# Twelve short products by zero in two feed-forward stages and four by zero ahead of two waits of TensorE

## The chip, the cores and the metric

The kernel runs on one core of a Trainium2 chip. The metric is the device time of one execution in microseconds (us). Its engines each run one queue of instructions in order: PE is TensorE (matrix products; PEld is its weight load), DVE is VectorE, ACT is ScalarE, POOL is GpSimd, SP is SyncE, which here issues the DMAs.

## What is computed

A two-layer decoder trunk over 256 positions of width 1024: layer 0 is a gated linear recurrence and a SwiGLU feed-forward, layer 1 is attention on shared keys and values and a second SwiGLU feed-forward; each is preceded by an RMS norm whose shift and scale come from a conditioning vector. Cut to what matters here:

```python
def rmsnorm(x, g):
    return x * lax.rsqrt(jnp.mean(x * x, axis=-1, keepdims=True) + RMS_EPS) * g

def swiglu(h, w_gate, w_up, w_down):          # 1024 -> 2816 -> 1024
    return (jax.nn.silu(h @ w_gate) * (h @ w_up)) @ w_down

for l in range(2):
    if l == 1:
        kv = shared_kv(x, shift, scale, kv_norm, w_kv)
    h = modulate(rmsnorm(x, norm_mix[l]), sh_m, sc_m)
    x = x + g_m * (rglru_mixer(h, ...) if l == 0 else moba_mixer(h, w_q, w_o, *kv, rel_bias))
    h = modulate(rmsnorm(x, norm_ffn[l]), sh_f, sc_f)
    x = x + g_f * swiglu(h, w_gate[l], w_up[l], w_down[l])
return rmsnorm(x, final_norm)
```

## The kernel before

**Products.** Activations lie transposed, 128 channels by 256 positions a tile. Most 128x128x256 products are done split: weight and activation are each cut into a high part and a rest (`whi`, `wlo` and `h`, `l`; ACT makes the high part, L439, DVE the rest, L440), and `mm3` issues three products in the fp32r format, high by high, high by rest, rest by high (L387 to L389). A product of plain float32 operands (L449, L544) comes as two records in the trace. Two feed-forwards, `f0` and `f1`, are built by `ffn`: `f_g`, 32 tiles (four output tiles `g00` to `g03`, k = 0 to 7) on the not yet normed input, while the sum of squares `f_st` (L544, five products against a tile of ones) is taken; then `f_p`, 320 tiles (ten steps i of two halves q, two j, eight k); then `f_d`, 176 tiles (eight outputs m, 22 k). `f_g` of `f0` is plain float32 (L449), that of `f1` is split. Steps of `f_p` are multiplied into `f` and split into `ah` and `al` (L606, L607) for `f_d`. Between the feed-forwards stand `kp`, `vp`, `qp` (keys, values, queries), the scores, `op` (probabilities by values) and `ao` (output projection); ahead of `f0`, `wo` (output projection of the recurrence) and `sh_f0`, a conditioning vector by 64 narrow float32 products on the PE (L477).

**Order.** Nothing of the order is written by hand. Every operation is handed to a planner, `Plan` (L93), with a rank: its number in the program, plus an amount by engine and name out of two tables, `KN` and `PRIO`. `Plan.run` (L153) keeps a clock for each engine and places, step by step, the ready operation that can start first, and among those the one of lowest rank; SBUF and PSUM slots (four for `whi`, four for `wlo`, four for raw weights, three for rows of conditioning weights `mraw`, eight PSUM banks) are given out in the same pass. The result is one fixed order for each engine; at run time an engine waits at the instruction that stands first in its queue, whatever stands behind it. One operation more, or one that takes longer in the planner's clock, can so move others on all engines.

Of the kernel before, what the change touches and what calls it, by code (L numbers as in the profile page):

```python
# [318 lines left out]
def build(tc, t):  # L319
    nc = tc.nc  # L320
    ctx = ExitStack()
    with ctx:
# [17 lines left out]
        slots("mraw", MRN, D)  # L340
        pool.tile([P, 16], F32, name="shift", tag="shift")
        slots("t2", T2N, 2 * S, KN["t2r"])
# [39 lines left out]

        def mm3(cost, out, wh, wl, xh, xl, start, stop, R, Wr, skip=False):
            def fn():
                o = out()
                h_, l_, a_, b_ = wh(), wl(), xh(), xl()
                nc.tensor.matmul(o, h_, a_, start=start, stop=False, skip_group_check=skip)  # L387
                nc.tensor.matmul(o, h_, b_, start=False, stop=False, skip_group_check=skip)  # L388
                nc.tensor.matmul(o, l_, a_, start=False, stop=stop, skip_group_check=skip)  # L389
            return pe(cost, fn, R, Wr)  # L390

# [18 lines left out]
        ones = own([P, P], "ones")  # L410
        dve(P, 0.0005, lambda: nc.vector.memset(ones.ap, 1.0), (), (ones,))
        warm = own([P, 1], "warm")
# [29 lines left out]

        def gemm(out, key, wu, o, xu, start, stop, skip=False, w=P, n=S, cost=0.3275):

            ps, c = out
            hi, lo = wu
            xh, xl, xo = xu
            if hi is None:
                pe(n * 0.0016875 + 0.002, lambda: nc.tensor.matmul(  # L449
                    ps.ap[:, c:c + n], lo.ap[:, o:o + w], xh.ap[:, xo:xo + n], start=start, stop=stop,  # L450
                    skip_group_check=skip), (lo, xh if n > S else (xh, xo)), ((ps, key),))
                return
            mm3(cost, lambda: ps.ap[:, c:c + n], lambda: hi.ap[:, o:o + w], lambda: lo.ap[:, o:o + w],
                lambda: xh.ap[:, xo:xo + n], lambda: xl.ap[:, xo:xo + n], start, stop,
                (hi, lo) + ((xh, xl) if n > S else ((xh, xo), (xl, xo))), ((ps, key),), skip)

# [8 lines left out]
        def mod_cols_pe(name, src, bias, g=None):  # L465

            ps = PS(name + "_ps")
            for u in range(4):
                raw = pl.buf("raw", f"{name}_r{u}")
                load(raw, CU, lambda raw=raw: raw.ap, src[u])  # L470
                for kk in range(2):
                    k = 2 * u + kk

                    def fn(k=k, kk=kk, raw=raw):
                        for q in range(4):
                            o = kk * D + q * S
                            nc.tensor.matmul(ps.ap[32 * q:32 * q + 32, :S], csr.ap[:, 32 * k:32 * k + 32],  # L477
                                             raw.ap[:, o:o + S], start=(k == 0), stop=(k == KC - 1),
                                             tile_position=(0, 32 * q))
                    pe(0.52, fn, (raw, csr), (ps,))  # L480
# [214 lines left out]
        def head_front(h):  # L695
# [43 lines left out]
            vv_.append(v_)  # L739

        def head_y(h):
            if h < NYH:
                ps = xps[NH_LRU + h]
            else:
                pl.bias = KN["ypsum"]
                ynat = h >= NH_LRU - 0
                wu = unit(t["win_y"][h - NYH], 2048, f"wiy{h}", ynat)
                ps = PS(f"yb{h}")
                pl.bias = KN["y"]
                for j in range(2):  # L750
                    for k in range(KC):
                        gemm((ps, j * S), 0, wu, (j * KC + k) * P, (hf[k], hf[k], 0) if ynat else hx(h0, k), k == 0,
                             k == KC - 1)
            pl.bias = KN["y"]
            y_ = T2(f"y{h}")
            act(2 * S, lambda: nc.scalar.activation(y_.ap, ps.ap, AF.Copy), (ps,), (y_,))
            ys.append(y_)
# [90 lines left out]
        def ffn(l, xs, a, sh, g, name, rates):  # L848
# [9 lines left out]
            shc = None if nat else shift_cols(sh, name)  # L858
            gp0 = [PS(f"{name}_g0{i}") for i in range(4)]
            wu = None  # L860
            for k in range(KC):
# [28 lines left out]
            for i in range(1, FT // 2):  # L890
                pq = [PS(f"{name}_p{i}{q}") for q in range(2)]
                wq = [unit(t[f"ffb{l}"][2 * (i - 1) + q], 2048, f"{name}b{i}{q}") for q in range(2)]
                if i == 1:
                    for k in range(KC):
                        for q in range(2):
                            for j in range(2):
                                gemm((pq[q], j * S), 0, wq[q], (j * KC + k) * P, hx(h, k), k == 0 and j == 0,
                                     k == KC - 1, skip=True)
                else:
                    for q in range(2):  # L900
                        for j in range(2):
                            for k in range(KC):
                                gemm((pq[q], j * S), 0, wq[q], (j * KC + k) * P, hx(h, k), k == 0, k == KC - 1)
                step(0)
# [6 lines left out]
            for m in range(KC):  # L911
                ps = PS(f"{name}_d{m}")
                for half in range(2):
                    wu = unit(t[f"ffc{l}"][2 * m + half], 11 * P, f"{name}c{m}{half}")
                    for kk in range(11):
                        k = half * 11 + kk
                        gemm((ps, 0), 0, wu, kk * P, hx(aa, k), k == 0, k == FT - 1)
                step(1)
# [172 lines left out]
        for u in range(4):  # L1091
# [3 lines left out]
            for m in range(KC):  # L1095
                for k in range(2):
                    gemm((acc[m // 2], (m % 2) * S), 0, wu, k * 1024 + m * P, (oh, ol, k * S),
                         u == 0 and k == 0 and m % 2 == 0, u == 3 and k == 1, skip=True)
        x3 = [residual(x2[k], acc[k // 2], (k % 2) * S, 0, mods["g_m1"], k, "x3") for k in range(KC)]

# [136 lines left out]
```

## Time and profile before

| | |
|---|---|
| time, three runs | 610.31, 613.24, 615.05 us; median 613.24 us |
| the profiled execution's own time | 608.61 us |
| its span, first to last instruction | 606.8 us |
| PE busy | 585.9 us, 97% |
| DVE, ACT busy | 471.8 us (78%), 340.6 us (56%) |
| DMA | 162.94 MB, mean 269 GB/s |
| f0, its products of f_p and f_d | 152 to 329 us of the span |
| f1, its products of f_p and f_d | 430 to 598 us of the span |

The profiled execution is one of its own and lies 4.6 us below the median of the three runs. A row of the trace gives the start within the span, the busy time, the engine, the line and operation, output and input, the shape and the count; in square brackets the idle time of the engine ahead of it and what ended it.

### The profile page before, as it was taken

Reading aid. Unit: us, or ns where it says so; the run is one execution under the profiler, and the core shown is the slowest. Engines: PE = TensorE matmul, PEld = TensorE weight load, DVE = VectorE, ACT = ScalarE, POOL = GpSimd, SP = SyncE. Lnnn points to the kernel's source line nnn. Section 1 sums busy time; section 2 is a strip of 40 time slices with the busy share of each in tenths; the row PEclk is TensorE's granted clock in tenths of the full one; section 3 lists DMA queues with packets and bytes.
Section 4 is the critical chain, followed back from the end, with each engine's and each line's share of the span. In section 5 each row is a group of like instructions: output and inputs, shape, how many; then the busy total and the mean of one; then the engine's idle time right before and its main releaser. Section 6 shows DMA issues by size and latency. Waiting matters only on the chain.

```text
span 606.8 us, 11423 instructions
## 1 busy us (share of the span) xinstructions
PE 585.9 (97%) x4706; PEld 563.2 (93%) x4706; DVE 471.8 (78%) x743; ACT 340.6 (56%) x509; POOL 1.2 (0%) x10
## 2 busy tenths in 40 slices
PE   3999989999999999999999999998999999999996
PEld 1999868998999999999999889998999999999996
DVE  6998788977997898788878969889997654545542
ACT  6537898718653443343336899747664444434432
POOL 0000000000000000000000000000000000000000
PEclk9999999999999999999999999999999999999999
DMA  8996999795988899798979538786686654445501
GB/s 307 353 339 239 332 355 355 278 383 224 350 312 323 336 348 323 257 334 315 377 295 357 203 143 322 282 332 245 218 306 274 214 203 165 144 144 192 191 1 70
DMA packets 33362, 162.94 MB, mean 269 GB/s; under 512 B 3700, under 2 KB 4893, under 8 KB 23966
## 3 DMA queue, kind: packets, MB, share of 16 engines
q1 hardware_dynamic: 33310, 162.21, 72.2%
q8 instruction: 37, 0.61, 0.4%
q14 instruction: 15, 0.12, 0.1%
HBM read 161.14 MB, written 1.06 MB: 267 GB/s over the span
## 4 chain that ended last, share of the span: by engine, by line
PE 63%; DMA 18%; DVE 12%; ACT 3%; issue 3%; SPq 0%; DVEq 0%; ACTq 0%
PE ps_f_p L388 11%; PE ps_f_p L387 11%; PE ps_f_p L389 11%; PE ps_f_d L388 3%; PE ps_f_d L389 3%; PE ps_f_d L387 3%; PE ps_ga L449 3%; DMA mraw_mr_sh_kv_m__2730<-in_kvmod 2%; DVE wlo_f0c_l L440 2%; DMA raw_sh_f_r<-in_modp 1%; DMA mraw_mr_g_m_m__3469<-in_mod 1%; DMA raw_wix<-in_win_x 1%; PE ps_qp L389 1%; PE ps_qp L388 1%; PE ps_qp L387 1%
## 5 line engine op out<-in xcount | busy, mean ns | idle before, releaser
L388 PE MATMUL ps_f_p<-t_f_l,whi_f0b_h 128*128 128x256 f32 x320 | 89.7, 280 | 0.0
L387 PE MATMUL ps_f_p<-t_f_h,whi_f0b_h 128*128 128x256 f32 x320 | 89.5, 280 | 0.0
L389 PE MATMUL ps_f_p<-t_f_h,wlo_f0b_l 128*128 128x256 f32 x320 | 89.3, 279 | 0.0
L389 PE MATMUL ps_f_p<-t_f_h,wlo_f1b_l 128*128 128x256 f32 x320 | 88.5, 276 | 0.0
L387 PE MATMUL ps_f_p<-t_f_h,whi_f1b_h 128*128 128x256 f32 x320 | 88.4, 276 | 0.0
L388 PE MATMUL ps_f_p<-t_f_l,whi_f1b_h 128*128 128x256 f32 x320 | 88.4, 276 | 0.0
L388 PEld LDWEIGHTS ps_f_p<-t_f_l,whi_f0b_h 128*128 128x128 f32 x320 | 60.1, 188 | 0.2 <-DVE t_f_l L568 0.2
L387 PEld LDWEIGHTS ps_f_p<-t_f_h,whi_f0b_h 128*128 128x128 f32 x320 | 60.2, 188 | 0.0
L389 PEld LDWEIGHTS ps_f_p<-t_f_h,wlo_f1b_l 128*128 128x128 f32 x320 | 60.1, 188 | 0.1
L388 PEld LDWEIGHTS ps_f_p<-t_f_l,whi_f1b_h 128*128 128x128 f32 x320 | 60.1, 188 | 0.0
L387 PEld LDWEIGHTS ps_f_p<-t_f_h,whi_f1b_h 128*128 128x128 f32 x320 | 60.1, 188 | 0.0
L389 PEld LDWEIGHTS ps_f_p<-t_f_h,wlo_f0b_l 128*128 128x128 f32 x320 | 59.8, 187 | 0.0
L440 DVE TENSOR_TENSOR wlo_f1b_l<-raw_f1b_r,whi_f1b_h 128x2048 fp32r<-128x2048 f32 x20 | 45.6, 2289 | 18.1 <-ACT whi_f1b_h L439 18.1
L439 ACT ACTIVATE whi_f1b_h<-raw_f1b_r 128x2048 fp32r<-128x2048 f32 x20 | 38.2, 1912 | 24.8 <-issue 11.9
L439 ACT ACTIVATE whi_f0b_h<-raw_f0b_r 128x2048 fp32r<-128x2048 f32 x20 | 38.2, 1910 | 21.5 <-issue 19.1
L388 PE MATMUL ps_f_d<-t_f_al,whi_f0c_h 128*128 128x256 f32 x176 | 49.2, 280 | 0.8 <-DVE t_f_al L607 0.8
L389 PE MATMUL ps_f_d<-t_f_ah,wlo_f0c_l 128*128 128x256 f32 x176 | 49.3, 280 | 0.0
L387 PE MATMUL ps_f_d<-t_f_ah,whi_f0c_h 128*128 128x256 f32 x176 | 49.1, 279 | 0.0
L440 DVE TENSOR_TENSOR wlo_f0b_l<-raw_f0b_r,whi_f0b_h 128x2048 fp32r<-128x2048 f32 x20 | 45.6, 2287 | 4.2 <-ACT whi_f0b_h L439 4.1
L389 PE MATMUL ps_f_d<-t_f_ah,wlo_f1c_l 128*128 128x256 f32 x176 | 48.6, 276 | 0.0
L387 PE MATMUL ps_f_d<-t_f_ah,whi_f1c_h 128*128 128x256 f32 x176 | 48.6, 276 | 0.0
L388 PE MATMUL ps_f_d<-t_f_al,whi_f1c_h 128*128 128x256 f32 x176 | 48.6, 276 | 0.0
(469 smaller groups left out, 1661.3 us busy)
## 6 DMA issues: line engine op xcount, KB each, us to landing
raw_f0b_r<-in_ffb SPq DMA_DIRECT2D x20, 1024.0 KB, 6.9
raw_f1b_r<-in_ffb SPq DMA_DIRECT2D x20, 1024.0 KB, 4.9
raw_f0c_r<-in_ffc SPq DMA_DIRECT2D x16, 704.0 KB, 5.9
raw_f1c_r<-in_ffc SPq DMA_DIRECT2D x16, 704.0 KB, 4.0
raw_wix<-in_win_x SPq DMA_DIRECT2D x8, 768.0 KB, 6.7
raw_wout_r<-in_wout SPq DMA_DIRECT2D x5, 1024.0 KB, 9.9
raw_wiy_r<-in_win_y SPq DMA_DIRECT2D x4, 1024.0 KB, 6.0
raw_sh_f_r<-in_modp SPq DMA_DIRECT2D x4, 1024.0 KB, 6.1
```

Of the source, the lines that this page charges most:

```text
L387: nc.tensor.matmul(o, h_, a_, start=start, stop=False, skip_group_check=skip)
L388: nc.tensor.matmul(o, h_, b_, start=False, stop=False, skip_group_check=skip)
L389: nc.tensor.matmul(o, l_, a_, start=False, stop=stop, skip_group_check=skip)
L439: act(n - o, lambda: nc.scalar.activation(hi.ap[:, o:n], raw.ap[:, o:n], AF.Copy), (raw,), (hi,))
L440: tt(n - o, lambda: nc.vector.tensor_sub(lo.ap[:, o:n], raw.ap[:, o:n], hi.f[:, o:n]), (raw, hi), (lo,))
L449: pe(n * 0.0016875 + 0.002, lambda: nc.tensor.matmul(ps.ap[:, c:c + n], lo.ap[:, o:o + w], xh.ap[:, xo:xo + n], start=start, stop=stop, sk ...
```

## The change

Two tiles of zeros and ones exist already or are made at the start: 16 columns of an unused tile are set to zero (`zero`), beside `ones` (128x128). `mm3` gets a flag `lead`: with it, one plain float32 product of `ones` by the 16 columns of `zero` is issued ahead of the three products, and added into the first 16 columns of the same output (the sum is unchanged, since it adds zero). In each feed-forward six tiles have it: of `f_p` i = 1 at k = 5 (q = 0, j = 0) and i = 4, 7, 10 at k = 1 (q = 0, j = 0), of `f_d` m = 1 and 4 at k = 1. `between` issues four plain float32 products of `zero` by the identity (16x128) into a PSUM tile that is overwritten later: one ahead of `sh_f0`, after a product `yb` of the recurrence, one ahead of `f_g` of `f1`, after the last product of `ao`. Both carry a rank of 1000 less than their number. The tables are unchanged. Lines behind the edits move by 2 to 23.

```diff
-        def mm3(cost, out, wh, wl, xh, xl, start, stop, R, Wr, skip=False):
+        def mm3(cost, out, wh, wl, xh, xl, start, stop, R, Wr, skip=False, lead=False):
             def fn():
                 o = out()
+                if lead:
+                    nc.tensor.matmul(o[:, :16], ones.ap, zero.ap, start=False, stop=False, skip_group_check=True)
                 h_, l_, a_, b_ = wh(), wl(), xh(), xl()
                 nc.tensor.matmul(o, h_, a_, start=start, stop=False, skip_group_check=skip)
...
+        zero = pl.buf(None, "zero", tile=zt)
+
+        def fixed():
+            nc.vector.memset(ones.ap, 1.0)
+            nc.vector.memset(zero.ap, 0.0)
+        dve(P, 0.0005, fixed, (), (ones, zero))
...
+        def between(ps, last):
+
+            def fn():
+                for i in range(4):
+                    nc.tensor.matmul(ps.ap[0:16, :P], zero.ap, ident.ap, start=True, stop=True)
+            pe(0.05, fn, (zero, ident), ((ps, 0),), after=[last], rank=-1000)
...
+            if name == "sh_f0":
+                between(ps, ybs[2,0,2])
...
+            if l == 1:
+                between(gp0[0], ao_last)
...
                                 gemm((pq[q], j * S), 0, wq[q], (j * KC + k) * P, hx(h, k), k == 0 and j == 0,
-                                     k == KC - 1, skip=True)
+                                     k == KC - 1, skip=True, lead=k == 5 and q == 0 and j == 0)
...
-                                gemm((pq[q], j * S), 0, wq[q], (j * KC + k) * P, hx(h, k), k == 0, k == KC - 1)
+                                gemm((pq[q], j * S), 0, wq[q], (j * KC + k) * P, hx(h, k), k == 0, k == KC - 1,
+                                     skip=i in (4, 7, 10) and q == 0 and j == 0 and k == 1, lead=i in (4, 7, 10) and q == 0 and j == 0 and k == 1)
...
-                        gemm((ps, 0), 0, wu, kk * P, hx(aa, k), k == 0, k == FT - 1)
+                        gemm((ps, 0), 0, wu, kk * P, hx(aa, k), k == 0, k == FT - 1, skip=m in (1, 4) and k == 1, lead=m in (1, 4) and k == 1)
```

The planner's result moves with it. Three places, before and after.

First, ACT where `f0` ends and the keys begin. `whi_wv0` and `whi_wv4` are the high parts of the two weight units of the values, `n2_sq0` to `n2_sq7` the squares of the eight tiles for the norm that the keys need. Before:

```order
L439 ACTIVATE whi_wv0_h_3700<-raw_wv0_r_3612 128x2048
L595 ACTIVATE t1_kv_u1_h_3746<-kv_sh_172 128x2
L599 ACTIVATE t1_kv_u1_h_3746<-t1_f0x_1_3236,sc_kv_m_158 128x256
L595 ACTIVATE t1_kv_u2_h_3749<-kv_sh_172 128x2
L599 ACTIVATE t1_kv_u2_h_3749<-t1_f0x_2_3315,sc_kv_m_158 128x256
L530 ACTIVATE t1_n2_sq0_3767<-t1_f0x_0_3138 128x256
L530 ACTIVATE t1_n2_sq1_3769<-t1_f0x_1_3236 128x256
L530 ACTIVATE t1_n2_sq2_3771<-t1_f0x_2_3315 128x256
L530 ACTIVATE t1_n2_sq3_3773<-t1_f0x_3_3403 128x256
L530 ACTIVATE t1_n2_sq4_3775<-t1_f0x_4_3492 128x256
L439 ACTIVATE whi_wv4_h_3777<-raw_wv4_r_3644 128x2048
L530 ACTIVATE t1_n2_sq5_3797<-t1_f0x_5_3577 128x256
```

With the change:

```order
L446 ACTIVATE whi_wv0_h_3713<-raw_wv0_r_3584 128x2048
L446 ACTIVATE whi_wv4_h_3751<-raw_wv4_r_3629 128x2048
L546 ACTIVATE t1_n2_sq0_3759<-t1_f0x_0_3151 128x256
L546 ACTIVATE t1_n2_sq1_3763<-t1_f0x_1_3245 128x256
L546 ACTIVATE t1_n2_sq2_3765<-t1_f0x_2_3331 128x256
L546 ACTIVATE t1_n2_sq3_3767<-t1_f0x_3_3424 128x256
```

All eight squares now stand behind the second high part. On the PE the five products `n_st` on those squares now stand right behind the last product of `f_d`, and all 96 products of `kp` behind them; before, 33 products of `kp` stood ahead of them, twelve of these between the last ones of `f_d`.

Second, DVE where attention ends and `f1` begins. `ol4` and `ol6` are the rests that the products of `ao` read (of heads 4 and 5, and 6 and 7), `mr_sh_f1_m` are rows of conditioning weights that come by DMA. Before:

```order
L440 TENSOR_TENSOR wlo_wo_3_l_4697<-raw_wo_3_r_4252,whi_wo_3_h_4495 128x2048
L1077 TENSOR_TENSOR t2_ol4_4573<-ps_op5_4703,t2_oh4_4552 128x256
L1077 TENSOR_TENSOR t2_ol6_4724<-ps_op6_4712,t2_oh6_4718 128x256
L462 SCALAR_TENSOR_TENSOR mraw_mr_sh_f1_m__4687,sh_f1_m_170<-mraw_mr_sh_f1_m__4687,csb_130 128x1024
L1077 TENSOR_TENSOR t2_ol6_4724<-ps_op7_4716,t2_oh6_4718 128x256
L462 SCALAR_TENSOR_TENSOR mraw_mr_sh_f1_m__4710,sh_f1_m_170<-mraw_mr_sh_f1_m__4710,csb_130 128x1024
```

With the change:

```order
L476 SCALAR_TENSOR_TENSOR mraw_mr_sh_f1_m__4672,sh_f1_m_170<-mraw_mr_sh_f1_m__4672,csb_130 128x1024
L1099 TENSOR_TENSOR t2_ol4_4710<-ps_op4_4541,t2_oh4_4700 128x256
L1099 TENSOR_TENSOR t2_ol4_4710<-ps_op5_4690,t2_oh4_4700 128x256
L476 SCALAR_TENSOR_TENSOR mraw_mr_sh_f1_m__4692,sh_f1_m_170<-mraw_mr_sh_f1_m__4692,csb_130 128x1024
L1099 TENSOR_TENSOR t2_ol6_4735<-ps_op6_4702,t2_oh6_4720 128x256
L476 SCALAR_TENSOR_TENSOR mraw_mr_sh_f1_m__4698,sh_f1_m_170<-mraw_mr_sh_f1_m__4698,csb_130 128x1024
L447 TENSOR_TENSOR wlo_f1a0_l_4752<-raw_f1a0_r_4396,whi_f1a0_h_4626 128x2048
L447 TENSOR_TENSOR wlo_f1a4_l_4775<-raw_f1a4_r_4504,whi_f1a4_h_4686 128x2048
L476 SCALAR_TENSOR_TENSOR mraw_mr_sh_f1_m__4750,sh_f1_m_170<-mraw_mr_sh_f1_m__4750,csb_130 128x1024
L1099 TENSOR_TENSOR t2_ol6_4735<-ps_op7_4793,t2_oh6_4720 128x256
L447 TENSOR_TENSOR wlo_f1b10_l_4801<-raw_f1b10_r_4644,whi_f1b10_h_4782 128x2048
```

Each rest now has a DMA's row ahead of it, the last one two units of weights besides. On the PE `op7` stands 36 products ahead of the end of `ao` (before: 84), and behind `ao` stand the four products of `between`, all five `f_st` and only then `f_g` (before: one `f_st`, twelve products of `f_g`, four `f_st`).

Third, PE and DVE at the end of `f_p` of `f1`: `g03` is the fourth output tile of `f_g`, `al0` the rest that the first products of `f_d` read. On the PE with the change:

```order
L391 MATMUL ps_f1_p101_6260<-t2_f1_h3_5170,wlo_f1b101_l_6170 128x256
L389 MATMUL ps_f1_g03_4952<-t1_f1_u7_h_5011,whi_f1a4_h_4686 128x258
L390 MATMUL ps_f1_g03_4952<-t1_f1_u7_l_5020,whi_f1a4_h_4686 128x258
L391 MATMUL ps_f1_g03_4952<-t1_f1_u7_h_5011,wlo_f1a4_l_4775 128x258
L389 MATMUL ps_f1_d0_6346<-t2_f1_ah0_6332,whi_f1c00_h_6204 128x256
```

On DVE there, with the change:

```order
L930 TENSOR_TENSOR t2_f1_f10_6320<-ps_f1_p101_6260,t2_f1_s10_6278 128x512
L905 TENSOR_TENSOR t1_f1_tu1_6324<-ps_f1_g03_4952,t1_f1_rstd_4897 128x256
L895 COPY f1_bs_195<-ps_f1_g03_4952 128x1
L907 SCALAR_TENSOR_TENSOR t2_f1_f0_5192<-t1_f1_tu1_6324,f1_bs_195,t1_f1_tg1_5176 128x256
L447 TENSOR_TENSOR wlo_f1c10_l_6330<-raw_f1c10_r_6133,whi_f1c10_h_6322 128x1408
L447 TENSOR_TENSOR wlo_f1c11_l_6336<-raw_f1c11_r_6196,whi_f1c11_h_6328 128x1408
L623 TENSOR_TENSOR t2_f1_al0_6340<-t2_f1_f0_5192,t2_f1_ah0_6332 128x512
```

Before, the last three products of `g03` stood at the start of `f1`, behind the first six of `f_p`, and `al0` on DVE ahead of the fourth step of `f_p`; now `g03` stands behind all of `f_p`, and `al0` behind it and two units of weights.

## Rows read from the trace of the kernel before

**Rows 1.** The page: the span and the first busy line.

```profile
span 606.8 us, 11423 instructions
PE 585.9 (97%) x4706; PEld 563.2 (93%) x4706; DVE 471.8 (78%) x743; ACT 340.6 (56%) x509; POOL 1.2 (0%) x10
```

**Rows 2.** Waits of the PE: who waited for whom, us in total, times, longest.

```profile
PE ps_f_st L544 <- DVE t_f_sq L539: 2.3, 2, 2.1
PE ps_sh_f_ps L477 <- DMA raw_sh_f_r<-in_modp: 2.2, 1, 2.2
PE ps_kp L388 <- DVE t_kv_u_l L601: 0.9, 1, 0.9
PE ps_f_d L388 <- DVE t_f_al L607: 0.8, 1, 0.8
```

**Rows 3.** Stretches of PE: us, busy (products), granted clock, DMA share, GB/s.

```profile
160.00:260.00 100.00, 100.00 (x852) 1.00 0.87 317
450.00:550.00 100.00, 100.00 (x884) 1.00 0.56 198
```

**Rows 4.** Timeline of PE: a short stop in f0 and one in f1.

```profile
273.15 0.38 PE L388 MATMUL ps_f_d<-t_f_al,whi_f0c_h 128*128 128x256 f32 x1 [0.78 <-DVE t_f_al L607]
...
434.31 0.38 PE L389 MATMUL ps_f_p<-t_f_h,wlo_f1b_l 128*128 128x256 f32 x1
```

**Rows 5.** Timeline of PE near the end: the narrowest float32 products.

```profile
598.76 0.50 PE L1121 MATMUL ps_n_st<-ones,t_n_sq 128*128 128x1 f32 x4
599.12 0.96 PE L1125 MATMUL ps_ty<-ident,t_y 128*128 128x128 f32 x7
```

**Rows 6.** Timeline of PE, DVE and ACT where f0 ends.

```profile
330.91 0.39 PE L388 MATMUL ps_kp<-t_kv_u_l,whi_wk_h 128*128 128x258 f32 x1 [0.93 <-DVE t_kv_u_l L601]
...
331.17 0.47 DVE L611 SCALAR_TENSOR_TENSOR t_f0x<-ps_f_d,g_f_m,t_x 128x256 f32<-128x256 f32 x1
331.56 1.47 DVE L539 TENSOR_TENSOR t_n_sq<-t_n_sq,t_n_sq 128x256 f32<-128x256 f32 x3
332.95 2.28 DVE L440 TENSOR_TENSOR wlo_wv_l<-raw_wv_r,whi_wv_h 128x2048 fp32r<-128x2048 f32 x1
...
329.83 1.91 ACT L439 ACTIVATE whi_wv_h<-raw_wv_r 128x2048 fp32r<-128x2048 f32 x1
331.68 1.15 ACT L530 ACTIVATE t_n_sq<-t_f0x 128x256 f32<-128x256 f32 x3
```

**Rows 7.** Timeline of PE, DVE and ACT where f1 begins.

```profile
416.02 0.67 PE L544 MATMUL ps_f_st<-t_f_sq,ones 128*128 128x256 f32 x2 [2.10 <-DVE t_f_sq L539]
...
406.27 1.22 DVE L462 SCALAR_TENSOR_TENSOR mraw_mr_sh_f_m__4687<-mraw_mr_sh_f_m__4687,csb 128x1024 f32<-128x1024 f32 x1 [2.12 <-DMA mraw_mr_sh_f_m__4687<-in_mod]
...
420.64 1.75 DVE L552 RECIPROCAL t_f_rstd<-t_f_rstd 128x256 f32<-128x256 f32 x1
...
417.03 1.32 ACT L530 ACTIVATE t_f_sq<-t_x 128x256 f32<-128x256 f32 x4
```

**Rows 8.** Timeline of DVE where f_p of f1 ends.

```profile
539.18 0.69 DVE L908 TENSOR_TENSOR t_f_f<-ps_f_p,t_f_s 128x512 f32<-128x512 f32 x1 [2.54 <-PE ps_f_p L389]
540.47 1.63 DVE L440 TENSOR_TENSOR wlo_f1c_l<-raw_f1c_r,whi_f1c_h 128x1408 fp32r<-128x1408 f32 x1 [0.59 <-ACT whi_f1c_h L439]
542.01 0.68 DVE L607 TENSOR_TENSOR t_f_al<-t_f_f,t_f_ah 128x512 fp32r<-128x512 f32 x1
```

**Rows 9.** Timeline of PE at the start: ten plain float32 products, twice.

```profile
14.22 4.63 PE L677 MATMUL ps_xb<-t_h,raw_wix 128*128 128x256 f32 x10 [4.41 <-ACT t_h L563]
...
20.65 2.32 PE L677 MATMUL ps_xb<-t_h,raw_wix 128*128 128x256 f32 x10
```

**Rows 10.** Timeline of ACT and PE where f0 begins.

```profile
134.54 3.30 ACT L591 ACTIVATE t_f_u_f<-t_x,sc_f_m 128x256 f32<-128x256 f32 x8 [1.03 <-DVE sc_f_m L515]
...
138.36 1.89 ACT L439 ACTIVATE whi_f0b_h<-raw_f0b_r 128x2048 fp32r<-128x2048 f32 x1
...
142.97 2.42 PE L544 MATMUL ps_f_st<-t_f_sq,ones 128*128 128x256 f32 x10 [0.20 <-DVE t_f_sq L539]
```

More of the change, by code (lines that the diff above doesn't have):

```diff
@@ L340, in build @@
         slots("mraw", MRN, D)
-        pool.tile([P, 16], F32, name="shift", tag="shift")
+        zt = pool.tile([P, 16], F32, name="shift", tag="shift")
         slots("t2", T2N, 2 * S, KN["t2r"])
@@ L389, in fn @@
                 nc.tensor.matmul(o, l_, a_, start=False, stop=stop, skip_group_check=skip)
-            return pe(cost, fn, R, Wr)
+            return pe(cost, fn, R + (ones, zero) if lead else R, Wr)
         vec = own([P, NV], "vec")
@@ L410, in build @@
         ones = own([P, P], "ones")
-        dve(P, 0.0005, lambda: nc.vector.memset(ones.ap, 1.0), (), (ones,))
+        zero = pl.buf(None, "zero", tile=zt)
[3 more added lines that the diff above has]
+        dve(P, 0.0005, fixed, (), (ones, zero))
         warm = own([P, 1], "warm")
@@ L441, in parts, with gemm @@
             return hi, lo
-        def gemm(out, key, wu, o, xu, start, stop, skip=False, w=P, n=S, cost=0.3275):
+        def gemm(out, key, wu, o, xu, start, stop, skip=False, w=P, n=S, cost=0.3275, lead=False):
             ps, c = out
@@ L454, in gemm @@
                 lambda: xh.ap[:, xo:xo + n], lambda: xl.ap[:, xo:xo + n], start, stop,
-                (hi, lo) + ((xh, xl) if n > S else ((xh, xo), (xl, xo))), ((ps, key),), skip)
+                (hi, lo) + ((xh, xl) if n > S else ((xh, xo), (xl, xo))), ((ps, key),), skip, lead)
+        def between(ps, last):
[3 more added lines that the diff above has]
+            pe(0.05, fn, (zero, ident), ((ps, 0),), after=[last], rank=-1000)
         def mod_col(dst, src, key, **k):
@@ L739, in head_front @@
             vv_.append(v_)
+        ybs = {}
         def head_y(h):
@@ L753, in head_y @@
                              k == KC - 1)
+                        ybs[h, j, k] = pl.ops[-1]
             pl.bias = KN["y"]
@@ L1098, in build @@
                          u == 0 and k == 0 and m % 2 == 0, u == 3 and k == 1, skip=True)
+        ao_last = pl.ops[-1]
         x3 = [residual(x2[k], acc[k // 2], (k % 2) * S, 0, mods["g_m1"], k, "x3") for k in range(KC)]
```

## The prediction, made before the change was run

> **What bounds the kernel now.** I read the page first: the PE is busy for 585.9 of 606.8 us, 97% [rows 1], so nearly every microsecond that the PE loses or gains is one of the span. Then the waits of the PE, to see what there is to win: behind the first 15 us only four count, 2.2 us for a DMA, 2.1 of 2.3 us at the start of `f1`, 0.9 and 0.8 us [rows 2], 6.0 us together. Two of these are the ones that get `between` ahead of them. Then stretches of the PE of equal length: in 100 us of `f0` 852 products are done, in 100 us of `f1` 884, both at a granted clock of 1.00 [rows 3]. That is 117.4 ns a product against 113.1, with the same shapes and no waits: the stream has two paces, 4.3 ns apart. The timeline shows where it changes: up to a stop at 434.31 us, where a product took 0.38 us instead of 0.28 us, the slow pace holds, behind it the fast one. A stop of the same look in `f0` at 273.15 us leaves the slow pace as it was [rows 4]. So an interruption can set the pace, and it holds until the next one; which pace follows is not in the rows.
>
> All sums are made against the profiled execution, 608.6 us (span 606.8 and 1.8 us around it). The median of the three runs is 613.2 us. What `f1` gains by its fast pace, 1449 products at 4.3 ns, is 6.2 us; an execution without it would take 614.8 us, so the runs shown may simply differ in pace.
>
> **The leads.** Twelve plain float32 products of 16 columns, two records each. The narrowest such products in the trace, 1 column, follow each other four in 0.50 us at most and 0.36 us from the first's start to the next group's [rows 5], about 0.11 us each. So 0.22 us a lead, 2.7 us for twelve. Bounds: nothing, if they slip into gaps of the stream; 0.43 us each, 5.2 us, if they cost what a full product of 256 columns does, 2.42 us for ten records [rows 10]. I take 2.7.
>
> What they may give back is the pace. In `f0` 1488 products of `f_p` and `f_d` run slow; the first lead stands behind 60 of them, so 1428 at 4.3 ns, 6.1 us, if a lead sets the fast pace. In `f1` the profiled execution has it already. Bounds: a gain of 6.1 us, or a loss of 6.2 us if the leads set the slow pace in `f1`. I take the gain: a lead is always the same interruption, with both operands long ready, so it should leave the same pace each time; and of the two stops it resembles the one at 434.31 us, a hold inside the stream with no idle time beside it, more than the wait of 0.78 us [rows 4].
>
> **`between`.** Eight records of 128 columns, at seven in 0.96 us [rows 5] about 1.1 us, inside waits of 2.2 and 2.1 us [rows 2]: nothing. If that cover went, 1.1 us each. The zero tile costs one small memset at the start, where the PE waits anyway.
>
> **The order.** The diff does not show it, but the planner's result moves, and the queues wait at what stands first. Four places cost something.
>
> *Start of `f0`.* Ahead of the eight `f_u_f` on ACT, and again between the fourth and the fifth, now stands a high part of 1.9 us [rows 10], and two rests stand ahead of the reciprocal on DVE. `f_u_f` began at 134.54 us on the arrival of its scale; now it ends later by what of the first high part does not fit before it, about 1.0 us, and the last squares by 0.3. I take 1.3 (0 to 2).
>
> *End of `f0`.* `f_d` ends at about 329.8 us; call this E. The second high part of the values starts only there, since its slot is freed by the last product of `f_d`: 1.9 us [rows 6]. All eight squares stand behind it: 0.33 us each when they run together (1.32 for four [rows 7]), the fourth done at E + 3.3. On DVE the residual (0.4 us) and the rest of that unit (2.2 us; it starts at about E + 2.4, behind the first one's rest) stand ahead of the three adds (1.4 us): E + 6.0. The PE has 0.7 us to do (`rp`) and then stands at `n_st`, 5.3 us. Before, twelve products of `kp` lay within `f_d` and 21 behind it, and the wait was 0.93 us [rows 6]. Net 4.4 (3 to 5.5).
>
> *End of attention, start of `f1`.* Before, `ol4` ran on DVE ahead of the row whose DMA landed at 406.27 us after a wait of 2.12 us [rows 7]; now both halves stand behind such a row, whose DMA is issued behind one megabyte of weights, while the PE wants them at about 403.5 us: some 2.5 us late, if the landing stays where it was. The last `ol6` has two rests of 2.2 us and one more row of 1.2 us [rows 6, 7] ahead of it, against 60 products, 7.1 us: 1 to 1.5 us late, since the row's DMA is again behind weights. In `f1` the high part (1.9 us) and the four last squares (1.32 us) [rows 6, 7] now stand behind `ao`'s end, `f_st` waits for them with no `f_g` among it, then `f_g` waits for a rest (2.2 us), the scale's last add behind it, a row (1.2), three `u_l` (1.2) and the reciprocal, 1.75 us [rows 7], ahead of the columns that its second product reads. Before, all of that ran beside 96 products of `f_g`. From the end of `ao` to the first product of `f_g` this makes 9 us, of which 2.1 were waited and 2.2 are `f_st`, and twelve products less are done: 5.5 us net if the attention part loses nothing, 10 with it. I take 7.5.
>
> *End of `f_p` in `f1`.* `f_d` now stands behind `g03`, whose result goes through DVE behind the last step's product: 0.69, then 0.4, 0.1 and 0.4, two rests at 1.55 and `al0` 0.68 us [rows 8]: 5.4 us behind the end of `f_p`, of which 0.4 us are the three products of `g03`, which are only moved. 5.0 us (4 to 5.5); before, no wait stands here [rows 2].
>
> Together 1.3 + 4.4 + 7.5 + 5.0 = 18.2 us (12.5 to 23).
>
> **The clock in the new waits.** At the start of the trace ten products took 4.63 us behind an idle time of 4.41 us, and 2.32 us at 20.65 us [rows 9]: half the pace, 1.2 for 2.4 GHz, though the row of the granted clock says 1.00. Behind the waits of 2.2 and 2.1 us it does not show. Three of the new waits are 4 to 5.3 us long, so each may cost up to 2.3 us; I take 3.0 in all (0 to 7), since the start differs: the PE had done little before.
>
> The Trainium skill ("TensorE: Matmul & The Clock Gate", section "Part 1: The HAM clock gate") says that the throttled clock is the default and that activity releases it. By that rule products by zero in a wait are worth something where the wait is long; for the two waits of before the trace does not bear it out, and the sum by the rule would be the same there, since nothing was lost. It does agree with the start.
>
> **The sum.** 608.6 + 2.7 + 18.2 + 3.0 − 6.1 = 626.4; I say 626 us.
>
> **Rivals.** *The pace is not the leads' to set* (it falls out anew each time, mostly slow): `f0` stays slow, 632 us, and `f1` falls back too, 639; for it speaks the stop at 273.15 us. *The waits are half as long*, because weights and rows land earlier than I have them and the engines catch up, and the clock does not fall: 608.6 + 2.7 + 9 − 6.1 = 614; for it speaks that each of these walks chains four or five durations. *Faster*: the pace decides, and the late work is hidden: 608.6 + 2.7 − 6.1 = 605; it needs all new waits together to stay under 1.9 us (607.1 is 1% under the median). Against it: at the end of `f_p` alone the queue holds 5 us of work that nothing on the PE covers.
>
> **Chances.** The forecast 0.45, the pace rival 0.25, half waits 0.20, faster 0.10. One per cent is about what a measurement of this kernel can tell, so the same is 607.1 to 619.4 us: most of the half-wait case, 0.17; slower 0.73; faster 0.10. The range goes from 613, the lower half-wait cases left out, to 640.
>
> **What would show it.** Right: in the waits of the PE a wait of about 5 us at `n_st` of the keys, one of 4 to 5 us at the first `f_d` of `f1` on `t_f_al`, several us at `f_st` and `f_g` of `f1`; about 884 products in 100 us in both feed-forwards; each lead two records of about 0.11 us. Wrong: waits in these places under 2 us, 852 products in 100 us of `f0` behind the first lead, or a stream that changes pace between two leads.

## The result and the profile after

The changed kernel takes 642.28 us (median of 4 runs, 640.97 to 643.13), before 611.93 us (4 runs, 610.31 to 615.05): ratio 1.053, 95% interval 1.049 to 1.058. Ratios and intervals here and below are formed from fast runs alone, without those over 1.5% above the fastest of the same kernel, so they can differ a little from the quotient of the medians, here 1.050. Slower was forecast, but 626 us, with a range up to 640; the result lies 2.3 us above that. The profiled execution took 642.7 us, its span is 640.9 us, 34.1 more than before [rows 1].

The page of the kernel after, span, first busy line and the granted clock in 40 slices:

```profile
span 640.9 us, 11526 instructions
...
PE 598.8 (93%) x4746; PEld 572.2 (89%) x4746; DVE 474.1 (74%) x744; ACT 341.4 (53%) x509; POOL 1.3 (0%) x10
...
PEclk9998999999999999999998999988999999979999
```

The PE stands still for 42.1 us of the span (before: 20.9), and is busy 12.9 us longer with the same products and some 5 us of products by zero. Two things to look for then: waits, and a clock that is not at 1.00 in several slices. The waits of the PE, kernel after (who waited for whom: us in total, times, longest):

```profile
PE ps_n_st L560 <- DVE t_n_sq L555: 8.3, 2, 5.0
...
PE ps_ao L390 <- DVE t_ol L1099: 3.5, 1, 3.5
PE ps_f_g L390 <- DVE t_f_u_l L613: 2.9, 1, 2.9
PE ps_f_d L389 <- ACT t_f_ah L622: 2.8, 1, 2.8
PE ps_wo L390 <- DVE t_ul L623: 2.5, 1, 2.5
...
PE ps_f_d L390 <- DVE t_f_al L623: 1.9, 1, 1.9
...
PE ps_f_g L389 <- ACT t_f_u_h L611: 1.2, 1, 1.2
PE ps_sh_f_ps L493 <- DMA raw_sh_f_r<-in_modp: 1.1, 1, 1.1
PE ps_op L1090 <- ACT t_pT L1082: 1.1, 1, 1.1
```

Against [rows 2] the large ones are new: 5.0 us at `n_st` of the keys, 1.1 and 3.5 us in the attention's end, 1.2 and 2.9 us at `f_g` of `f1`, 2.8 and 1.9 us at its first `f_d`, all in the three places that the forecast walked through, and 2.5 us in `wo`, which it did not. In `sh_f` the wait went from 2.2 to 1.1 us; the four products of `between` now lie in it. (Two other executions of these queues, the two fills below, wait 1.5 and 1.8 us there.)

Stretches of PE, kernel after, 10 us each (us, busy and products, granted clock, DMA share, GB/s), those around the large waits:

```profile
40.00:50.00 10.00, 7.85 (x51) 0.94 0.97 365
50.00:60.00 10.00, 10.00 (x61) 0.89 0.60 226
120.00:130.00 10.00, 7.49 (x54) 0.87 0.88 326
340.00:350.00 10.00, 10.00 (x68) 0.88 0.51 185
410.00:420.00 10.00, 5.49 (x33) 0.87 0.92 358
440.00:450.00 10.00, 9.44 (x66) 0.83 0.49 175
560.00:570.00 10.00, 5.30 (x39) 0.88 0.44 146
570.00:580.00 10.00, 10.00 (x70) 0.78 0.26 86
```

And the last of them more closely:

```profile
568.00:570.00 2.00, 1.17 (x5) 0.50 0.93 327
570.00:572.00 2.00, 2.00 (x12) 0.50 0.92 287
...
574.00:576.00 2.00, 2.00 (x17) 0.88 0.00 0
```

Behind these waits the granted clock goes to 0.50 (1.2 of 2.4 GHz) and stays there for some microseconds in which products are done at half the pace. Summed over all stretches of 10 us, (1 minus clock) times 10 us makes 12.2 us; before, it is 1.00 everywhere up to the last microsecond. That sum is not the loss itself, since part of it lies on the waits and 0.3 us on the end: the products done at the lower clock took an estimated 11.2 us longer than the same products at 1.00, from the times between their starts, 2.0 us of it in the first 80 us.

The pace, kernel after, 50 us in `f0` and in `f1`:

```profile
210.00:260.00 50.00, 50.00 (x444) 1.00 0.89 338
490.00:540.00 50.00, 50.00 (x444) 1.00 0.50 184
```

444 products in 50 us are the 884 in 100 us that only `f1` had before [rows 3]. Here is where it starts, at the second lead of `f0` (timeline of PE: start us, us, engine, line, operation):

```profile
196.40 0.28 PE L390 MATMUL ps_f_p<-t_f_l,whi_f0b_h 128*128 128x256 f32 x1
196.52 0.28 PE L391 MATMUL ps_f_p<-t_f_h,wlo_f0b_l 128*128 128x256 f32 x1
196.64 0.29 PE L387 MATMUL ps_f_p<-shift,ones 128*128 128x16 f32 x2
196.78 0.36 PE L389 MATMUL ps_f_p<-t_f_h,whi_f0b_h 128*128 128x256 f32 x1
196.98 0.28 PE L390 MATMUL ps_f_p<-t_f_l,whi_f0b_h 128*128 128x256 f32 x1
```

From 196.52 to 196.98 us it is 0.46 us instead of 0.23, so a lead costs 0.23 us. Ahead of it products start 0.118 us apart, behind it 0.113. Five of the twelve leads have the slow pace ahead of them. Behind three of these it is the fast one, behind two (the first of `f0` and the fifth of `f1`) still the slow one. No lead ends the fast pace.

### The profile page after: what moved, and what is told of

The parts are those of the page before. It is cut to its first block, busy times and chain, and to the rows that moved or that the text cites. A ratio compares the mean times of both kernels' runs of the same rounds, so it can differ in the third digit from the quotient of the medians.

```text
span 640.9 us, 11526 instructions
## 1 busy us (share of the span) xinstructions
PE 598.8 (93%) x4746; PEld 572.2 (89%) x4746; DVE 474.1 (74%) x744; ACT 341.4 (53%) x509; POOL 1.3 (0%) x10
## 5 line engine op out<-in xcount | busy, mean ns | idle before, releaser
L389 PE MATMUL ps_f_d<-t_f_ah,whi_f1c_h 128*128 128x256 f32 x176 | 50.3, 286 | 2.8 <-ACT t_f_ah L622 2.8
L390 PE MATMUL ps_f_d<-t_f_al,whi_f1c_h 128*128 128x256 f32 x176 | 50.2, 285 | 1.9 <-DVE t_f_al L623 1.9
L391 PE MATMUL ps_f_d<-t_f_ah,wlo_f1c_l 128*128 128x256 f32 x176 | 50.0, 284 | 0.0
```

## The experiments

All are named by what they keep or add; ratios are to the kernel before, run in the same rounds (its median was 614.1, 614.8 and 616.1 us in the three groups of rounds), with 95% intervals. The theory going in (A): the moved order is the loss, the products by zero are nearly free. Rival B: the products themselves, or what they do to the stream, are the loss.

**The leads alone, before's order** (`e1_leads`): the two `between` out, all else as in the change.

```diff
-            if name == "sh_f0":
-                between(ps, ybs[2,0,2])
...
-            if l == 1:
-                between(gp0[0], ao_last)
```

> The twelve leads alone, in the order of the kernel before (they are issued inside the functions that the planner places, without telling it). Theory A, the moved order is the cost: twelve leads at 0.226 us, 2.7 us, less the pace that they set; where ten of twelve leave the fast pace, as in the changed kernel, about 1200 products of f0 gain 4.4 ns, 5.3 us, so 608.6 + 2.7 - 5.3 = 606 us, and up to 611 if f1 keeps its slow pace in places; no new wait over 0.5 us and a granted clock of 1.00. Theory B, the products by zero are the cost by breaking into the stream: above 625 us.

Measured: 610.01 us (12 runs, 608.14 to 618.36), ratio 0.994 (0.990 to 0.998). Behind all twelve leads the pace is the fast one: 2857 products at 113 ns against 1505 before. Only two of them, the first and the fifth of `f0`, had the slow pace ahead; `f1` was fast before its first lead, as in the kernel before. Two things expected did not hold: the wait at `kp` is 1.9 us here (before: 0.9) and the one in `sh_f` 3.0, and behind both the granted clock falls to 0.50, at 332 and 80 us.

**`between` alone, before's order** (`e2_between`): no leads; the four products are issued within the operation that stands behind the wait, so the planner does not see them.

```diff
+                        if name == "sh_f0" and k == 0:
+                            for q in range(4):
+                                nc.tensor.matmul(ps.ap[0:16, :P], zero.ap, ident.ap, start=True, stop=True)
```

> The eight products ahead of the two waits alone, in the order of the kernel before (issued ahead of the first product that stands behind each wait). Theory A: they lie inside the waits of 2.2 and 2.1 us, which get shorter by 1 us each, and the time stays within 2 us of the kernel before, about 611 us. Theory C, they keep the clock up in executions where it falls behind one of these waits: 1 to 3 us faster than the kernel before, with a smaller spread. Theory B: slower by more than 5 us.

Measured: 614.85 us, ratio 1.000 (0.997 to 1.003). Nothing, as the forecast had it. The profiled execution runs nearly all its products at the slow pace, `f1` too: without leads the pace differs from one execution of the same queues to another.

**The order alone** (`e3_order`): the changed kernel without any product by zero; the planner still gets the operations.

```diff
-                for i in range(4):
-                    nc.tensor.matmul(ps.ap[0:16, :P], zero.ap, ident.ap, start=True, stop=True)
+                pass
...
-                if lead:
-                    nc.tensor.matmul(o[:, :16], ones.ap, zero.ap, start=False, stop=False, skip_group_check=True)
```

> The order of the changed kernel without any product by zero: the leads and the products ahead of the waits are left out, the planner is told the same as in the changed kernel. Theory A: the waits at wo, at n_st of the keys, at ao, at f_g and f_d of f1 are all there (some 20 us more than before) and the granted clock falls behind them (about 12 us), so 608.6 + 33 = 641, about 640 to 648 us, as f0 and f1 run mostly at the slow pace. Theory B: back near 612 us.

Measured: 643.28 us (638.87 to 646.90), ratio 1.047 (1.040 to 1.055). Waits of the PE in it:

```profile
PE ps_n_st L557 <- DVE t_n_sq L552: 7.7, 2, 4.9
...
PE ps_f_g L388 <- DVE t_f_u_l L610: 2.9, 1, 2.9
PE ps_f_d L387 <- ACT t_f_ah L619: 2.8, 1, 2.8
PE ps_wo L388 <- DVE t_ul L620: 2.5, 1, 2.5
```

They are the waits of the changed kernel but for the 3.5 us in `ao`, which are 0.6 us here, and the loss is, within the intervals, the whole loss. Its parts are not quite the same: this execution, the slowest of the four, has no leads to pay and runs nearly all products at the slow pace.

**The whole change, before's order** (`e4_both`): the leads of the first run and the products of the second.

```diff
+                    nc.tensor.matmul(o[:, :16], ones.ap, zero.ap, start=False, stop=False, skip_group_check=True)
...
+                        if name == "sh_f0" and k == 0:
+                            for q in range(4):
+                                nc.tensor.matmul(ps.ap[0:16, :P], zero.ap, ident.ap, start=True, stop=True)
```

> All products by zero of the change, leads and those ahead of the waits, in the order of the kernel before: the change without its move of the order. Theory A: 608.6 + 2.7 - 5.3 = 606 us, up to 611; waits and clock as before. Theory B: above 630 us, near the changed kernel's 642.

Measured: 611.54 us, ratio 1.001 (0.997 to 1.005). With these four A stands and B falls. One expectation is missed: waits and clock are not quite as before. The first `f_d` of `f0` waits twice, 1.6 us apart, and the granted clock falls to 0.50 behind it; in the run of `between` alone it does so behind waits of 1.1 and 1.2 us at the same place.

```profile
PE ps_f_d L390 <- DVE t_f_al L621: 1.2, 1, 1.2
PE ps_f_d L389 <- ACT t_f_ah L620: 0.8, 1, 0.8
```

**One number of the planner** (`e6_price`). The planner's result for each part shows which operation moves the order: leads alone and the second `between` alone leave the queues as before, the first `between` alone gives the whole new order. It stands on the PE's clock in the planner with 0.05 us.

```diff
-            pe(0.05, fn, (zero, ident), ((ps, 0),), after=[last], rank=-1000)
+            pe(0.01, fn, (zero, ident), ((ps, 0),), after=[last], rank=-1000)
```

> The whole change, with one number changed: the planner's price of `between` is 0.01 instead of 0.05 us. All products by zero are still done at the same places; against before's order only the four products at the first `between`, five rows of DVE and two DMAs move. Theory A (the order that the price of 0.05 makes is the loss): like the whole change in before's order, about 611.5 us (607 to 616), waits of the PE behind the first 50 us under 2.5 us. Rival B (products by zero at these places cost the time whatever the order): 635 us or more.

Measured: 612.87 us (12 runs), ratio 1.000 (0.995 to 1.005). The same products at the same places cost nothing when the queues stay. One wait is longer than expected, at the first `f_d` of `f0`, the place of the last run's fall, and the clock falls here too:

```profile
PE ps_f_d L389 <- ACT t_f_ah L622: 2.7, 1, 2.7
```

**Filling the waits, badly** (`e5_fill`). Are the falls of the clock a cost of their own? The changed kernel, with more products by zero in its waits.

```diff
+                for _ in range(ahead):
+                    nc.tensor.matmul(o[0:16, :P], zero.ap, ident.ap, start=True, stop=True, skip_group_check=True)
                 h_, l_, a_, b_ = wh(), wl(), xh(), xl()
                 nc.tensor.matmul(o, h_, a_, start=start, stop=False, skip_group_check=skip)
+                for _ in range(inside):
+                    nc.tensor.matmul(o[:, :16], ones.ap, zero.ap, start=False, stop=False, skip_group_check=True)
```

> The changed kernel with more products by zero, put into five of its long waits: 10 and 14 short ones behind the first product of a group in `wo` and `ao`, 34 of 128 columns ahead of `n_st` of the keys, 7 and 11 at the first `f_g` of `f1`, 19 and 7 at its first `f_d`; the order of every queue is that of the changed kernel, and what is computed is the same. Theory A (the granted clock falls because the PE stood still, and the falls cost about 10 us here): the operands arrive when they did, so the spaces between the real products stay (2.5, 5.0, 3.5, 1.2 and 2.9, 2.8 and 1.9 us), but the clock stays at 1.00 behind them: about 632 us (629 to 636). Rival B (the clock follows the moved work, or such short products do not hold it): the falls stay, 642 to 645 us.

Measured: 640.36 us (636.22 to 642.89), ratio 1.046 (1.036 to 1.056): neither 632 nor 642 to 645. The numbers of products were wrong: one of 128 columns is two records, 0.23 us, so 34 outlast the 5.0 us at the keys and 19 the 2.8 us at `f_d`; and the 14 in `ao` stood at a group that does not wait. What it shows all the same: at the unfilled wait of `ao` the clock fell (first row below), in `wo`, at the keys and at `f_d` it stayed at 1.00, and at `f_g`, filled in its second part with products of 16 columns, it fell (third row). It also fell where the PE did not wait at all: from 419.40 us the 14 products in `ao`, 28 records of 16 columns, follow each other for 3.2 us, which the profile counts as busy, and the clock is at 0.50 from 423.1 us on (second row). So standing still is not the only thing that lets it fall. Stretches of PE:

```profile
412.00:414.00 2.00, 2.00 (x11) 0.50 0.95 391
...
420.00:430.00 10.00, 9.53 (x67) 0.83 0.34 139
...
440.00:442.00 2.00, 2.00 (x11) 0.55 0.45 176
```

**Filling the waits, fitted** (`e10_fit`): 128 columns throughout, fewer than the waits hold, and at the group of `ao` that waits.

```diff
-                        for q in range(34):
+                        for q in range(16):
...
-                         inside=14 if (u, m, k) == (3, 0, 0) else 0)
+                         inside=13 if (u, m, k) == (2, 0, 0) else 0)
...
-                    nc.tensor.matmul(o[:, :16], ones.ap, zero.ap, start=False, stop=False, skip_group_check=True)
+                    nc.tensor.matmul(o[0:16, :P], zero.ap, ident.ap, start=False, stop=False, skip_group_check=True)
```

> The changed kernel with products by zero of 128 columns (two records, 0.23 us each) in its long waits, this time fewer than the waits hold, and at the head of the group of `ao` that really waits: 9 in `wo`, 16 ahead of `n_st` of the keys, 13 in `ao`, 4 and 11 at the first `f_g` of `f1`, 10 and 7 at its first `f_d`; the order of the queues is that of the changed kernel. Theory A (the clock falls where the PE stood still): the granted clock stays at 1.00 behind all of them, the real products stand where they stood, and the about 10 us that the falls cost behind the first 50 us are back: 632 us (629 to 636). Rival B (an execution of this order pays the same elsewhere, the falls are not the cost): 640 us or more.

Measured: 635.33 us (633.70 to 636.64), ratio 1.032 (1.027 to 1.038), against 1.053 for the change, as A has it; its span is 631.9 us, 9.0 less. Stretches of PE, those that answer to the falls of the changed kernel:

```profile
120.00:130.00 10.00, 9.56 (x82) 1.00 0.95 366
340.00:350.00 10.00, 10.00 (x81) 1.00 0.28 90
410.00:420.00 10.00, 9.46 (x75) 1.00 0.68 263
430.00:440.00 10.00, 9.63 (x82) 1.00 0.68 245
560.00:570.00 10.00, 9.63 (x79) 1.00 0.41 144
```

No fall is left up to the end of `f1`. Between the same products of the two traces it is shorter by 1.5 us in `wo`, 1.6 us from the last `f_d` to the first `kp`, 2.1 us in `ao`, 0.3 us in `f_g` and 2.5 us in `f_d` of `f1`: 8.0 us that the clock had cost. At `f_g` little came back, because the PE, now faster, waits there for the next `u_l`. Of the 9.0 us of the span, 3.5 lie ahead of the first product of `sh_f`, where nothing was filled; of the 8.0 behind it 1.4 us go again at `f_st` of `f0` and 1.2 at the first `f_p` of `f1`, where the PE now comes too early. So the fill is worth some 5.5 us of the span, though the clock had cost 8.0 between the products. The Trainium skill ("TensorE: Matmul & The Clock Gate", section "Part 1: The HAM clock gate") says that the throttled clock is the default and that activity releases it; these rows agree, 1.00 with products by zero in the waits and 0.50 without.

**Waits of chosen length** (`e11_stall`, `e12_stall2`): what a wait costs when nothing is moved. Between two products by zero stand so many memsets of GpSimd on the tile that the second one reads.

```diff
+                if stall:
+                    nc.tensor.matmul(o[:, :16], ones.ap, zero.ap, start=False, stop=False, skip_group_check=True)
+                    for _ in range(stall):
+                        nc.gpsimd.memset(zero.ap, 0.0)
+                    nc.tensor.matmul(o[:, :16], ones.ap, zero.ap, start=False, stop=False, skip_group_check=True)
```

> Before's order, no `between`; at eleven places inside the feed-forwards a pair of products by zero with a chain of 8 to 44 small memsets of GpSimd between them, for which the second one waits: waits of the PE of an estimated 0.8 to 3 us, 21 us together, that come from nothing else and move nothing else. What is computed is unchanged. Theory A (a wait of 2.5 us or more lets the clock fall, and the fall costs 1.6 to 3.4 us beside the wait itself): 0.50 in the granted clock behind the four longest, about 645 us. Rival B (the falls belong to the moved order, a wait costs its own length only): 636 us, clock 1.00.

> As the run with chains of 8 to 44 memsets, with chains of 20 to 70 at the same places, 30 us of waits by the same estimate, and other lengths at each place. Theory A: eight falls to 0.50, about 664 us, and each fall follows the length of its wait and not the place. Rival B: 646 us, clock 1.00 throughout.

Measured: 684.99 and 724.68 us (2 runs each). Both times are far off, since a memset took 0.17 us, over twice the estimate, so the waits are longer than meant: from 1.7 to 12.2 us between the two products. They serve better so, and they settle the question: the falls come in before's order too, so B is wrong that they belong to the moved order. Stretches of PE in the first kernel: a wait of 2.75 us in `f0` and what stands behind it, the same length in `f1`, and one of 7.8 us:

```profile
222.00:225.00 3.00, 0.51 (x7) 1.00 0.86 284
225.00:227.00 2.00, 2.00 (x17) 1.00 0.85 260
565.00:568.00 3.00, 0.66 (x7) 1.00 0.72 240
568.00:570.00 2.00, 1.85 (x8) 0.54 0.00 0
...
533.00:541.00 8.00, 0.43 (x5) 0.78 0.66 247
541.00:543.00 2.00, 2.00 (x9) 0.50 0.13 53
```

And in the second one behind a wait of 12.2 us:

```profile
504.50:506.50 2.00, 1.71 (x8) 0.50 0.00 0
506.50:508.50 2.00, 2.00 (x11) 0.50 0.00 0
```

Of 22 waits the one of 1.7 us had no fall behind it, of the two of 2.75 us one had, all 19 of 3.7 us and more had. These lengths run from the start of one product to the start of the next; the idle time of the PE, which the lists of waits give, is 0.25 us less, 2.49 us for the two of 2.75, about that of the wait in `wo`. By that measure, in all the traces of this case between the first 35 and the last 12 us, every wait of 2.8 us or more that no product fills has a fall, and of the 17 of 1.9 to 2.7 us with no longer one just ahead 11 have one. A fall cost 11 to 25 products at 213 ns, 1.1 to 2.4 us, 1.75 us in the mean, and that does not grow with the wait: 1.8 and 2.1 us behind the two of 12.2 us, 2.3 and 1.1 us behind the two of 3.75.

**The leads twice and three times** (`e9_twice`, `e13_thrice`), before's order, no `between`.

```diff
-                    nc.tensor.matmul(o[:, :16], ones.ap, zero.ap, start=False, stop=False, skip_group_check=True)
+                    for _ in range(2):
+                        nc.tensor.matmul(o[:, :16], ones.ap, zero.ap, start=False, stop=False, skip_group_check=True)
```

> Before's order, no `between`, each of the twelve leads issued twice. Theory A (a lead costs its two records, 0.226 us, and the first one sets the pace): 2.7 us more than with single leads, 612.7 us, and 0.68 us from the start of the product ahead of a pair to that of the second one behind it, instead of 0.45 us. Rival B (the price of a lead is the change of kind, plain float32 between fp32r products, paid once): 610 us, the gap stays under 0.5 us. If the leads do not set the pace but only break the stream, two should change no more than one.

> Before's order, no `between`, each of the twelve leads issued three times. Theory A (whether a lead leaves the fast pace hangs on how many stand together: with two none of twelve did, with one about half did from the slow pace): if an odd number does it, products 113.3 ns apart behind most of the triples and 8.3 us for the leads at 0.23 us each, 615.5 us. Rival B (more than one together leaves the slow pace): 117.8 ns throughout, about 624 us.

Measured: 621.08 us (ratio 1.016, 1.008 to 1.023) with two, 615.07 us (1.002, 0.997 to 1.006) with three. Stretches of PE in `f0` with two:

```profile
210.00:260.00 50.00, 50.00 (x428) 1.00 0.86 311
```

and with three:

```profile
210.00:260.00 50.00, 50.00 (x443) 1.00 0.91 336
```

The price is as expected, 0.23 us for each product: 0.68 us from the product ahead to the second one behind a pair, 0.90 us with three. But all twelve pairs have the slow pace ahead and the slow pace behind them. Of the triples four met the slow pace and two of these, the second of `f0` and of `f1`, turned it to the fast one; the other eight met the fast one and kept it. Two cost 11 us more than one: 2.7 us for the leads, the rest for the fast pace that is gone. The first run's forecast of 612.7 us missed that; the forecast for three, 615.5 us, held. So a lead does not only interrupt the stream: one or three can set the fast pace, two did not. Why is open. It goes with the place: over the traces with single leads, those at i = 4 that met the slow pace turned it in 6 of 6 cases, those at i = 1 in 6 of 12, those at m = 4 in 3 of 5, those at m = 1 in 1 of 4.

**More leads** (`e8_more`): one more in `wo`, two each in `kp` and `ao`, one more at i = 1.

```diff
+                     skip=m == 1 and k in (2, 6), lead=m == 1 and k in (2, 6))
...
+                         lead=m == 4 and k == 1 and u in (1, 3))
```

> Before's order, no `between`, the twelve leads and seven more: one in `wo`, two in `kp`, two in `ao`, one more at i = 1, k = 5 of each feed-forward. Theory A (each lead behind slow products has about an even chance to set the fast pace, none sets the slow one): under 700 products at the slow pace instead of 1151, 2 us or more gained, 1.6 us paid at 0.226 us a lead: 609.5 us (607 to 612). Rival B (what the twelve leads gained was the luck of the executions): no fewer slow products, 611.6 us and the ratio at 1.00.

Measured: 609.55 us, ratio 0.996 (0.992 to 1.000): not better than the twelve alone. The time is the one A forecast, but by luck, since its reason did not hold: 1470 products ran slow, not under 700. Behind the five leads outside the feed-forwards the pace stayed slow.

## Why the prediction was wrong

Each term of the sum, against the profiled execution of the changed kernel (us):

| term | forecast | measured | from |
|---|---|---|---|
| leads | 2.7 | 2.7 | 12 times 0.23 |
| `between` | 0 | 0 | run on its own: ratio 1.000 |
| start of `f0` | 1.3 | 0.6 | last `wo` to first `f_p`, 17.1 against 16.6 |
| end of `f0`, `n_st` of the keys | 4.4 | 4.0 | 4.96 less 0.93 |
| end of attention, start of `f1` | 7.5 | 7.5 | waits of 9.6 less 2.1 |
| end of `f_p` in `f1` | 5.0 | 4.7 | 2.83 and 1.87 |
| pace | −6.1 | −3.9 | 2381 products at 113 ns instead of 1505 |
| clock behind the waits | 3.0 | 9.2 | 11.2 less 2.0 in the first 80 us |
| `wo` | not in the sum | 2.5 | the wait for `t_ul` |
| first 80 us | not in the sum | 5.2 | first product of `sh_f` behind the wait: 82.89 against 77.67 |

With the measured terms the sum is 641.1 us, against 642.7.

**What held.** That the loss comes from the queues and not from the products; the three large places and their lengths, within half a microsecond each; the leads' price and that `between` is hidden. Inside the places not all is as forecast: at `f_d` of `f1` 2.8 of the 4.7 us are a wait for `ah0` on ACT, not for `al0`, and `f_st` of `f1` waits 0.5 us instead of several.

**The step that failed is "The clock in the new waits".** It had the mechanism and its bound for one wait right (up to 2.3 us; the stalls give 1.1 to 2.4), but it put 3.0 us where some 9 were lost: it took 1.0 us where a fall costs about 1.75, and counted "three of the new waits" where six falls came. Those behind the waits in `wo`, at `n_st`, in `ao` and at `f_g` cost an estimated 1.5 to 1.7 us each, the one behind the two waits of 2.83 and 1.87 us 2.7, and the sixth, behind the wait of 2.15 us in the first 50 us, 2.0. The argument that the waits of 2.2 and 2.1 us of before show no fall did not carry: the same length can go either way, as the two stalls of 2.75 us show. The 8.0 us between the products of the fitted fill in place of 3.0 lift the forecast from 626 to 631; what is left is the wait in `wo` (2.5), the smaller gain by the pace (2.2) and the first 80 us (5.2), all three below.

**A place not walked.** On DVE the rest `t_ul` of the third head, which the products of `wo` read, stood ahead of the following before and now stands behind four rows of conditioning weights and the rests of two weight units. The last three rows, timeline of DVE, kernel after:

```profile
122.04 1.22 DVE L476 SCALAR_TENSOR_TENSOR mraw_mr_sc_f_m__1318<-mraw_mr_sc_f_m__1318,csb 128x1024 f32<-128x1024 f32 x1
...
123.18 1.22 DVE L476 SCALAR_TENSOR_TENSOR mraw_mr_sc_f_m__1337<-mraw_mr_sc_f_m__1337,csb 128x1024 f32<-128x1024 f32 x1
...
124.33 1.22 DVE L476 SCALAR_TENSOR_TENSOR mraw_mr_sc_f_m__1356<-mraw_mr_sc_f_m__1356,csb 128x1024 f32<-128x1024 f32 x1
...
125.47 1.89 DVE L623 TENSOR_TENSOR t_ul<-t_y,t_uh 128x512 fp32r<-128x512 f32 x3
```

The move stands in the planner's result and could have been walked as the other four were; the 2.5 us wait and the fall behind it were not in the sum.

**The first 80 us** are not the change's: two other executions of the same queues there reach that product at 77.55 and 79.41 us (the two fills), and over all the traces it comes between 77 and 83 us whatever the queues. The sum was built on one execution, 608.6 us. The profiled execution of before was 3.3 us below its median and the one of after at its own, which is why the profiles differ by 34.1 us and the medians by 30.4.

**The pace.** The choice of the faster stop as the model held: no lead ended the fast pace, and the leads alone make the kernel 0.6% faster. That is small: with `between` beside them the ratio is 1.001 and 1.000. The gain was smaller than forecast because a lead behind the slow pace does not always change it; in the changed kernel three of five did. The rival that "the pace is not the leads' to set" falls in part with the runs of one, two and three leads. It is right that without leads the pace falls out anew: `f1` was fast in the profiled execution of before and slow in that of `between` alone.

**The other rivals.** Half waits did not come: the engines did not catch up at any of the three places. One wait is the execution's own, though: the 3.45 us in `ao` were 3.4 us again in the first fill, but 0.6 us in the run of the order alone: that the 7.5 us were met so closely is in part luck. The faster case would have needed the order to stay, and then the time comes near it: 610.0 us for the leads alone, where 605 was worked out.

What stays open: what sets the two paces, and what decides whether a wait of 1.9 to 2.7 us, or two of about 1 us close together, are followed by a fall.

## What to carry to other kernels

Where a planner sets the order, an added operation's price to the planner can matter more than its price on the chip: compare the queues first, and add helpers of this kind behind the planner's back or at a price that leaves the order alone. When a PE at full load gets new waits, charge each one of 2.8 us or more with about 1.75 us besides its length; of those of 1.9 to 2.7 us 11 in 17 had a fall here. Or fill the waits with products of 128 columns in fitting number; the clock held with those of 16 columns in `wo` and fell with them in `ao` and at `f_g`. A short plain float32 product between fp32r ones is worth a try where a stream runs at the slower of two paces, since here one for 0.23 us could buy 4.5 ns on each of several hundred products behind it; the whole kernel gained 0.6% at best.

## What was not expected of the hardware

- A fall of the clock costs about the same, 1.1 to 2.4 us, behind a wait of 3.7 us and one of 12.2 us.
- The clock can fall without a wait: it did behind 28 records of 16 columns that followed each other for 3.2 us.
- A memset of 128x16 on GpSimd in a chain takes 0.17 us; the estimate ahead of the first of those two runs, 21 us for 274 of them, had under 0.08.
- fp32r products of 128x128x256 run in one of two steady paces, 113.3 and 117.8 ns apart. One or three short float32 products can move the stream from the slow to the fast one; two did so in none of twelve places, and single ones in 16 of the 27 at which they met the slow one in the feed-forwards.
